# First loads of X and weights reordered onto one queue, the second weight chunk in halves, and the input norm in hooks, in a two-layer decoder step

## The chip, the cores and the metric

The kernel runs on one core of a Trainium2 chip. A core has five engines that run at the same time, each with its own instruction stream: TensorE (PE, matrix products into PSUM), VectorE (DVE), ScalarE (ACT), GpSimd (POOL) and SyncE (SP), which here only issues transfers. ACT can issue transfers too. Transfers of all queues run on the core's 16 DMA engines. The metric is the device time of one execution in microseconds; lower is better. Three runs of the kernel before took 632.65, 633.56 and 635.03 us, median 633.56.

## The reference

One inference step of a two-layer decoder, for a prompt of 256 tokens and 8 sample tokens that share the weights, so 264 columns in all. Layer 0 is block-sparse attention beside a gated mixer, layer 1 is stick-breaking attention beside a pooling mixer, and each layer ends in a feed-forward block with a short convolution. What bears on this change is the start of layer 0:

```python
def rmsnorm(x, g):
    xf = x.astype(jnp.float32)
    y = xf * lax.rsqrt(jnp.mean(xf * xf, axis=-1, keepdims=True) + EPS)
    return (y * g).astype(x.dtype)
...
    h = rmsnorm(x, norm_g)
    z = h @ w_in
    q, k, v, bu, bv = jnp.split(z, [A_WIDTH, 2 * A_WIDTH, 3 * A_WIDTH, 3 * A_WIDTH + B_WIDTH], axis=-1)
    q = rope_partial(q.reshape(B, T, A_HEADS, HEAD_DIM), pos)
    k = rope_partial(k.reshape(B, T, A_HEADS, HEAD_DIM), pos)
```

The norm's factor is one number per token, so it can be applied behind the product: the kernel multiplies X by the gain, projects, and multiplies the result by the factor R.

## The kernel before

Everything is held transposed: 128 features on the partitions, 264 tokens along the row. X is eight such tiles (`XG`, with the gain's 8 columns in front). Each weight matrix is cut into 128x128 blocks, and all blocks of the whole step lie in memory in the order in which PE uses them, as one stream of chunks: the first six chunks (0 to 5) hold 8 blocks (512 KB), all later ones 16 (1 MB). Three buffers hold chunks (`rawp`), so chunk n+3 can be loaded when chunk n has been used up.

For accuracy every product is made of three passes. A weight chunk is split, 8 blocks at a time, into a high part `wh` (a rounded copy, on ACT, L311) and a low part `wl` (the difference, on DVE, L312). X times gain is split in the same way into `xg_h` (ACT, L378) and `xg_l` (DVE, L379). A block then takes three matmuls: `wh` with `xg_h` (L334), `wh` with `xg_l` (L335), `wl` with `xg_h` (L336).

The input projection `in0` makes 20 output tiles (four each of q, k, bv, bu, v). The four q tiles go first and together: for each of the first five X tiles the four blocks of q0 to q3, then the other three X tiles for one q tile after the other. So chunk 0 is used with X tiles 0 and 1, chunk 1 with X tiles 2 and 3, chunk 2 with X tile 4 and then all the others. The four q tiles fill the four PSUM buffers `mm` of the projections. The first k tile can start only when a q tile has been evacuated, and evacuating q needs the rope factors times R (L612 to L614, then L634 to L640), so it needs the norm.

The opening. ACT issues X in four transfers (tiles 0, 1, 2 to 3, 4 to 7; L348 to L350), SP issues chunk 0 in three (2, 2 and 4 blocks; L351 to L354) and chunks 1 and 2 whole (L355, L356). Then ACT loads its function table (L357). Eight matmuls on a tile of ones, 512 columns each, keep PE at work until data is there (L358 to L362). The loop at L595 splits the three pieces of chunk 0 (`piece`, both parts on DVE, L308 and L309), makes the eight operand tiles and, two tiles behind (`SQL` 2), the squares of X for the norm (`nrm.add`: a square on ACT, L391, added up on POOL, L400 and L403). All of these are kept in the order in which they are written (`keep_in_program_order`). Behind the loop stand chunk 3, the rope table, the split of chunk 1, chunk 4, the small constants, and `nrm.finish()`: two matmuls with a matrix of ones add up the squares over the features (L411), and ACT makes R as Ln and Exp (L413, L414). Then come the three rope factors, and then the projection.

Instructions that aren't kept in order are placed by a scheduler that works on a model of the times. Within `run` (L315) hooks, small functions with a due time in units of 8 blocks, put the attention's work between the matmuls: page loads of the K cache from `KL` on (L788), score matmuls S (L654 to L657), sample scores `sc` (L456), transposes (L675), and so on. The transfers of K and V pages, of the chunks and of the small tables all go through SP's queue in one order, and a transfer whose buffer isn't free holds up all that stand behind it. Transfers also share eight completion counters in turn, so each waits for the landing of the transfer eight before it.

Of the kernel before, what the change touches and what calls it, by code (L numbers as in the profile page):

```python
# [11 lines left out]
BF16 = mybir.dt.bfloat16  # L12
I32 = mybir.dt.int32
AF = mybir.ActivationFunctionType
# [4 lines left out]
P = 128  # L19
# [18 lines left out]
KQ = 5  # L38
PINM = 8
SQL = 2  # L40
XD = (1, 2, 4, 8)
WARM = 8
YG = (2, 5)
# [19 lines left out]
MSK = 4.5  # L63
KL = 0
VL = 9
# [161 lines left out]
def tile_decoder_step(ctx: ExitStack, tc: tile.TileContext, a):  # L227
# [49 lines left out]
    NT = _NB // 8  # L277
    raws, splits = {}, {}

    def raw(ci):  # L280
        if ci not in raws:
            n = _CHUNKS[ci] * P
            r = rawp.tile([P, n], F32, tag="raw", name=f"raw{ci}")
            o = coff[ci] * P * P
            src = a["w"][o:o + P * n].rearrange("(p f) -> p f", p=P)
            raws[ci] = r
            if ci == 0:
                return lambda c, e: nc.sync.dma_start(r[:, c * P:e * P], src[:, c * P:e * P])
            nc.sync.dma_start(r, src)
        return raws[ci]  # L290
# [4 lines left out]
    def split(t):  # L295
        for tt in range(len(splits), min(t + (LOOK if pos[0] else 0), NT - 1) + 1):
            ci = chunk_of[tt]
            for c in range(ci, min(ci + 3, len(_CHUNKS))):
                raw(c)
            o = (tt * 8 - coff[ci]) * P  # L300
# [10 lines left out]
            s.activation(h, src, AF.Copy)  # L311
# [45 lines left out]
    s.preload_act_table_set("natural_log_exp_and_others")  # L357
    warm = con.tile([P, 512], BF16, name="warm")  # L358
    v.memset(warm, 1.0)
    pw = at("warm")  # L360
    for i in range(WARM):
        tc.keep_in_program_order(pe.matmul(pw, warm[:, :P], warm, start=i == 0, stop=i == WARM - 1))  # L362

    def late(dst, src):
        tc.keep_in_program_order(nc.sync.dma_start(dst, src))

# [222 lines left out]

    xg = [mv(f"xg_0{i}") for i in range(2)]  # L590
    nrm = Norm("n0", True)
    piece = split(0)
    pieces = [(0, 2), (2, 4), (4, 8)]
    for m in range(KD):
        if pieces:  # L595
            piece(*pieces.pop(0))
        operand_tile(xg[m // 4], m, X[:, m, :], GAIN[:, m:m + 1], pin=m < PINM)
        if m >= SQL:
            nrm.add(m - SQL, pin=m < PINM)
    for m in range(KD - SQL, KD):  # L600
        nrm.add(m)
    raw(3)
    late(CS, a["rope"].rearrange("p (c t) -> p c t", c=2))
    split(1)
# [7 lines left out]
    v.tensor_tensor(rope[:, 0, :], CS[:, 0, :], R, ALU.mult)  # L612
    v.scalar_tensor_tensor(rope[:, 2, :], CS[:, 1, :], SCALE, R, ALU.mult, ALU.mult)
    v.tensor_tensor(rope[:, 1, :], CS[:, 1, :], R, ALU.mult)  # L614

# [13 lines left out]
    def in0_evac(m, o):  # L629
# [11 lines left out]
        else:  # L641
            v.tensor_tensor({"v": v4, "bv": bv4, "bu": bu4}[n][:, t, :], o, R, ALU.mult)

# [424 lines left out]
```

## Time and profile before

| | |
|---|---|
| median of the three runs | 633.56 us |
| the profiled execution's own time | 632.96 us |
| its span, first to last instruction | 630.9 us |
| PE busy | 611.6 us, 97% |
| PE weight loads busy | 583.2 us, 92% |
| DVE busy | 413.2 us, 65% |
| ACT busy | 343.8 us, 54% |
| POOL busy | 82.5 us, 13% |
| mean granted PE clock | 0.994 |
| DMA | 121.42 MB, mean 192 GB/s |

Times in the profile's views are counted from the first instruction. The profiled execution took 2.06 us more than its span. "Busy" is time in which an engine had an instruction in work; "idle before" names what ended a wait, the releaser. A matmul's row lasts longer than the step to the next one, since matmuls are pipelined. Queue q1 carries SP's transfers and q10 ACT's.

### The profile page before, as it was taken

What the parts mean: (1) busy time and instruction counts of PE and PEld (TensorE: products, weight loads), DVE (VectorE), ACT (ScalarE), POOL (GpSimd) and SP (SyncE); (2) the same over time, 40 slices, a digit from 0 to 9 for tenths busy, and PEclk for the clock granted to TensorE, in tenths of its full rate; (3) what the DMA queues carried; (4) which work ended last, traced back from release to release, by engine and by line L of the source; (5) the groups of instructions that cost most, each with busy time, mean ns of one, the idle gap of its engine ahead of it and who ended that gap; (6) DMA issues with size and microseconds to landing.
All of it is one profiled execution on the core that took longest, in us unless ns stands there. A gap on an engine that the chain in (4) does not pass through costs nothing.

```text
span 630.9 us, 12406 instructions
## 1 busy us (share of the span) xinstructions
PE 611.6 (97%) x4956; PEld 583.2 (92%) x4956; DVE 413.2 (65%) x690; ACT 343.8 (54%) x608; POOL 82.5 (13%) x111
## 2 busy tenths in 40 slices
PE   7899999998999999999999999999899999999994
PEld 5887997998999999999998886999899999999994
DVE  6895674959966676655654674396996667664442
ACT  6448653667665555644442664366766555564441
POOL 3320132324000000010110000032400000001021
PEclk8999999999999999999999999999999999999998
DMA  7995673543555455795477679354355545554501
GB/s 271 324 414 223 238 262 72 182 156 132 200 201 180 161 195 198 228 382 202 179 189 300 230 117 112 129 172 169 128 200 200 179 166 191 201 165 177 200 1 70
DMA packets 40971, 121.42 MB, mean 192 GB/s; under 512 B 17490, under 2 KB 18642, under 8 KB 29522
## 3 DMA queue, kind: packets, MB, share of 16 engines
q1 hardware_dynamic: 40050, 119.15, 57.2%
q10 hardware_dynamic: 864, 1.49, 0.7%
q8 instruction: 39, 0.64, 0.4%
q14 instruction: 18, 0.15, 0.1%
HBM read 116.68 MB, written 3.94 MB: 191 GB/s over the span
## 4 chain that ended last, share of the span: by engine, by line
PE 90%; DVE 4%; ACT 2%; DMA 2%; issue 1%; POOL 1%; SPq 0%; DVEq 0%; ACTq 0%; POOLq 0%
PE mm L334 27%; PE mm L335 27%; PE mm L336 26%; DMA raw<-in_w 2%; DVE wl L312 1%; PE pv_l L470 1%; PE sc L456 1%; ACT wh L311 1%; PE Z L880 1%; PE Z L868 1%; PE pav L499 1%; DVE xn_l L379 1%; PE S L655 1%; PE S L654 1%; PE po_l L483 1%
## 5 line engine op out<-in xcount | busy, mean ns | idle before, releaser
L312 DVE TENSOR_TENSOR wl<-raw,wh 128x1024 fp32r<-128x1024 f32 x183 | 229.1, 1253 | 135.1 <-ACT wh L311 135.1
L311 ACT ACTIVATE wh<-raw 128x1024 fp32r<-128x1024 f32 x183 | 193.4, 1059 | 204.9 <-PE mm L335 187.6
L335 PE MATMUL mm<-xn_l,wh 128*128 128x264 f32 x544 | 154.4, 284 | 0.0
L336 PE MATMUL mm<-xn_h,wl 128*128 128x264 f32 x544 | 154.1, 283 | 0.0
L334 PE MATMUL mm<-xn_h,wh 128*128 128x264 f32 x544 | 153.9, 283 | 0.0
L334 PEld LDWEIGHTS mm<-xn_h,wh 128*128 128x128 f32 x544 | 102.3, 188 | 0.0
L335 PEld LDWEIGHTS mm<-xn_l,wh 128*128 128x128 f32 x544 | 102.3, 188 | 0.0
L336 PEld LDWEIGHTS mm<-xn_h,wl 128*128 128x128 f32 x544 | 102.2, 188 | 0.0
L335 PE MATMUL mm<-a_l,wh 128*128 128x264 f32 x352 | 99.9, 284 | 0.0
L336 PE MATMUL mm<-a_h,wl 128*128 128x264 f32 x352 | 99.7, 283 | 0.0
L334 PE MATMUL mm<-a_h,wh 128*128 128x264 f32 x352 | 99.5, 284 | 0.0
L335 PEld LDWEIGHTS mm<-a_l,wh 128*128 128x128 f32 x352 | 66.2, 188 | 0.0
L336 PEld LDWEIGHTS mm<-a_h,wl 128*128 128x128 f32 x352 | 66.2, 188 | 0.0
L334 PEld LDWEIGHTS mm<-a_h,wh 128*128 128x128 f32 x352 | 66.1, 188 | 0.0
L334 PE MATMUL mm<-xg_h,wh 128*128 128x264 f32 x160 | 46.9, 300 | 4.2 <-ACT wh L311 2.5
L334 PE MATMUL mm<-xg_f_h,wh 128*128 128x264 f32 x160 | 46.2, 289 | 4.5 <-DVE wk L558 4.3
L335 PE MATMUL mm<-xg_l,wh 128*128 128x264 f32 x160 | 45.6, 291 | 0.0
L336 PE MATMUL mm<-xg_f_h,wl 128*128 128x264 f32 x160 | 45.3, 283 | 0.0
L335 PE MATMUL mm<-xg_f_l,wh 128*128 128x264 f32 x160 | 45.3, 283 | 0.0
L336 PE MATMUL mm<-xg_h,wl 128*128 128x264 f32 x160 | 45.2, 294 | 0.1
L334 PE MATMUL mm<-xg_n_h,wh 128*128 128x264 f32 x128 | 37.9, 296 | 0.0
L335 PE MATMUL mm<-xg_n_l,wh 128*128 128x264 f32 x128 | 37.0, 289 | 0.0
(257 smaller groups left out, 1088.5 us busy)
## 6 DMA issues: line engine op xcount, KB each, us to landing
raw<-in_w SPq DMA_DIRECT2D x89, 1024.0 KB, 4.8
K<-in_kt SPq DMA_DIRECT2D x32, 256.0 KB, 6.2
V<-in_vp SPq DMA_DIRECT2D x32, 256.0 KB, 5.4
raw<-in_w SPq DMA_DIRECT2D x5, 512.0 KB, 5.1
CST<-in_cst SPq DMA_DIRECT2D x1, 560.0 KB, 4.7
XG<-in_x ACTq DMA_DIRECT2D x1, 528.0 KB, 7.7
out_k<-k SPq DMA_DIRECT2D x1, 528.0 KB, 8.7
out_v<-v SPq DMA_DIRECT2D x1, 528.0 KB, 3.0
```

What stands on the lines that cost most here:

```text
L311: s.activation(h, src, AF.Copy)
L312: v.tensor_tensor(l, src, h.bitcast(F32), ALU.subtract)
L334: pe.matmul(o, h[:, c:c + P], xh, start=first, stop=False)
L335: pe.matmul(o, h[:, c:c + P], xl, start=False, stop=False)
L336: pe.matmul(o, l[:, c:c + P], xh, start=False, stop=left[m] == 0)
L379: j = v.scalar_tensor_tensor(l, src, gain, h.bitcast(F32), ALU.mult, ALU.subtract)
L456: pe.matmul(ps[32 * t:32 * t + 32, :PAST].rearrange("p (g k) -> p g k", g=NPG), qz[:, t, sq, :], kt[sq][:, :, t * P:(t + 1) * P], start=sq ...
L470: pe.matmul(pv[32 * j:32 * j + 32, :], pz[:, pg, sq, :], vtiles[sq][:, pg, :], start=pg == 0, stop=pg == NPG - 1)
L483: pe.matmul(po[:, t * NS:(t + 1) * NS], msk[:, gr, 2 * t:2 * t + 2, :].rearrange("p h d -> p (h d)"), cst("selS")[:, gr * NS:(gr + 1) * NS ...
L499: pe.matmul(o, vt[:, 0, h * HD:(h + 1) * HD], w[:, :SEQ], start=True, stop=False)
L654: pe.matmul(ps[:, 0:P], qh[:, 0:P], kh[:, 0:P], start=True, stop=False, skip_group_check=True)
L655: pe.matmul(ps[:, P:384], qh[:, P:SEQ], kh[:, 0:SEQ], start=False, stop=False, skip_group_check=True)
```

## The change

All loads of the opening but one go through SP's queue, in an order written out: X tile 0 (with the gain), chunk 0 in three pieces, X tile 2, chunk 1's first half, X tile 3, its second half, X tile 4, chunk 2, X tiles 5 to 7, chunk 3. X tile 1 alone is issued by ACT, now behind its function table. Chunk 1 is split in two pieces of 4 blocks, like chunk 0's pieces; the last piece of chunk 0 and both of chunk 1 have their high part made on ACT instead of DVE. The squares follow three tiles behind the operand tiles (`SQL` 3); the last three and `nrm.finish()` with the rope factors (`norm0`) become hooks in the projection, due at 0 and 1.5. The warm-up is ten matmuls of 256 columns, and the K pages' loads start at hook 1 instead of 0 (`KL`). As built, the matmuls of the norm's sum stand on PE behind the last q matmul and ahead of the first k matmul; before, they stood between q matmuls. The first two pairs of score matmuls stand inside the fourth k tile, where they stood in the first bv tile. From the second half of the projection on, the instructions of all engines stand in the order in which they stood before.

```diff
-PINM = 8
-SQL = 2
-XD = (1, 2, 4, 8)
-WARM = 8
+SQL = 3
+WARM = 10
...
-KL = 0
+KL = 1
...
-            if ci == 0:
-                return lambda c, e: nc.sync.dma_start(r[:, c * P:e * P], src[:, c * P:e * P])
+            if ci < 2:
+                return lambda c, e: late(r[:, c * P:e * P], src[:, c * P:e * P])
...
             for c in range(ci, min(ci + 3, len(_CHUNKS))):
-                raw(c)
+                if tt > 1:
+                    raw(c)
...
-            if tt == 0:
-                def piece(c, e, h=h, l=l, src=src):
+            if tt < 2:
+                def piece(c, e, act, h=h, l=l, src=src):
                     c, e = c * P, e * P
-                    tc.keep_in_program_order(v.tensor_copy(h[:, c:e], src[:, c:e]))
+                    hh = s.activation(h[:, c:e], src[:, c:e], AF.Copy) if act else v.tensor_copy(h[:, c:e], src[:, c:e])
+                    tc.keep_in_program_order(hh)
                     tc.keep_in_program_order(v.tensor_tensor(l[:, c:e], src[:, c:e], h[:, c:e].bitcast(F32), ALU.subtract))
-                return piece
+                pieces.append(piece)
+                continue
...
-    xcut = [0] + [KD + e * T for e in XD]
-    for b, e in zip(xcut, xcut[1:]):
-        nc.scalar.dma_start(XG[:, b:e], a["x"][:, b:e])
-    part = raw(0)
-    part(0, 2)
-    part(2, 4)
-    part(4, 8)
-    raw(1)
+    def xload(m, e, eng=None):
+        b, e = KD + m * T if m else 0, KD + e * T
+        tc.keep_in_program_order((eng or nc.sync).dma_start(XG[:, b:e], a["x"][:, b:e]))
+
+    s.preload_act_table_set("natural_log_exp_and_others")
+    xload(1, 2, nc.scalar)
+    part0, part1 = raw(0), raw(1)
+    xload(0, 1)
+    part0(0, 2)
+    part0(2, 4)
+    part0(4, 8)
+    xload(2, 3)
+    part1(0, 4)
+    xload(3, 4)
+    part1(4, 8)
+    xload(4, 5)
     raw(2)
-    s.preload_act_table_set("natural_log_exp_and_others")
-    warm = con.tile([P, 512], BF16, name="warm")
+    xload(5, 8)
+    raw(3)
+    warm = con.tile([P, 256], BF16, name="warm")
...
+    split(1)
+    todo = [(0, 0, 2, False), (0, 2, 4, False), (0, 4, 8, True), None, (1, 0, 4, True), (1, 4, 8, True)]
+    def weights(n):
+        for x in [todo.pop(0) for _ in range(min(n, len(todo)))]:
+            if x:
+                pieces[x[0]](*x[1:])
+    weights(1)
     nrm = Norm("n0", True)
-    piece = split(0)
-    pieces = [(0, 2), (2, 4), (4, 8)]
     for m in range(KD):
-        if pieces:
-            piece(*pieces.pop(0))
-        operand_tile(xg[m // 4], m, X[:, m, :], GAIN[:, m:m + 1], pin=m < PINM)
+        operand_tile(xg[m // 4], m, X[:, m, :], GAIN[:, m:m + 1], pin=True)
+        weights(2 if m == 0 else 1)
         if m >= SQL:
-            nrm.add(m - SQL, pin=m < PINM)
-    for m in range(KD - SQL, KD):
-        nrm.add(m)
-    raw(3)
+            nrm.add(m - SQL, pin=True)
+        if m == 4:
+            split(2)
...
-    R = nrm.finish()
...
+    def norm0():
+        R = nrm.finish()
+        R0.append(R)
...
+    for m in range(KD - SQL, KD):
+        hk.at(0, nrm.add, m)
+    hk.at(1.5, norm0)
```

More of the change, by code (lines that the diff above doesn't have):

```diff
@@ L277, in tile_decoder_step @@
     NT = _NB // 8
-    raws, splits = {}, {}
+    raws, splits, pieces = {}, {}, []
     def raw(ci):
@@ L361, in tile_decoder_step @@
     for i in range(WARM):
-        tc.keep_in_program_order(pe.matmul(pw, warm[:, :P], warm, start=i == 0, stop=i == WARM - 1))
-    def late(dst, src):
-        tc.keep_in_program_order(nc.sync.dma_start(dst, src))
+        tc.keep_in_program_order(pe.matmul(pw[:, :256], warm[:, :P], warm, start=i == 0, stop=i == WARM - 1))
     ident = cst("ident")
@@ L608, in tile_decoder_step @@
     late(CST, a["cst"])
-    R = nrm.finish()
     rope = f4("rope")
-    v.tensor_tensor(rope[:, 0, :], CS[:, 0, :], R, ALU.mult)
-    v.scalar_tensor_tensor(rope[:, 2, :], CS[:, 1, :], SCALE, R, ALU.mult, ALU.mult)
-    v.tensor_tensor(rope[:, 1, :], CS[:, 1, :], R, ALU.mult)
+    R0 = []
+    def norm0():
+        R = nrm.finish()
+        R0.append(R)
+        v.tensor_tensor(rope[:, 0, :], CS[:, 0, :], R, ALU.mult)
+        v.scalar_tensor_tensor(rope[:, 2, :], CS[:, 1, :], SCALE, R, ALU.mult, ALU.mult)
+        v.tensor_tensor(rope[:, 1, :], CS[:, 1, :], R, ALU.mult)
     maskb0 = con.tile([P, P], BF16, name="maskb0")
@@ L641, in in0_evac @@
         else:
-            v.tensor_tensor({"v": v4, "bv": bv4, "bu": bu4}[n][:, t, :], o, R, ALU.mult)
+            v.tensor_tensor({"v": v4, "bv": bv4, "bu": bu4}[n][:, t, :], o, R0[0], ALU.mult)
     ktiles, kload = page_list(a["kt0"], "K0")
```

3 lines of the change are left out of this document (2 added, 1 removed).

## The prediction

> **What bounds the kernel now.** I read the waits of TensorE (PE) first, to see where it stands still, then the chain of waits and the order of time over the first 25 us, then the stages and the DMA counts.
>
> The order of time on PE, columns start, duration, engine, line, operation, and in brackets the idle time with its releaser:
> ```profile
> 1.46 3.60 PE L362 MATMUL warm<-warm 128*128 128x512 bf16 x8 [1.46 <-DVE warm L359]
> 4.50 0.99 PE L334 MATMUL mm<-xg_h,wh 128*128 128x264 f32 x2
> ...
> 10.81 0.76 PE L334 MATMUL mm<-xg_h,wh 128*128 128x264 f32 x4 [2.52 <-ACT wh L311]
> ...
> 18.92 0.61 PE L411 MATMUL ns_n<-acc_n,ones 128*128 128x264 f32 x2
> 19.36 0.61 PE L411 MATMUL ns_n<-sq_n,ones 128*128 128x264 f32 x2
> ...
> 22.48 0.28 PE L335 MATMUL mm<-xg_l,wh 128*128 128x264 f32 x1
> 22.60 0.28 PE L336 MATMUL mm<-xg_h,wl 128*128 128x264 f32 x1
> 24.54 0.36 PE L334 MATMUL mm<-xg_h,wh 128*128 128x264 f32 x1 [1.66 <-DVE q L636]
> ```
> PE stands still twice after its first real matmul at 4.50: 2.52 us until the second weight chunk is split, and 1.66 us at 24.54, where the first k tile wants a PSUM buffer that a q tile still holds, because its evacuation needs the norm. A matmul starts every 0.12 us (22.48 to 22.60). From 24.54 PE runs on, so all that the change can win in the opening is how far it moves that 24.54 forward.
>
> The chain of waits, columns start, duration, piece:
> ```profile
> 2.13 7.55 DMA raw<-in_w
> 9.70 1.06 ACT wh L311
> 10.76 0.41 ACT xg_h L378
> 11.17 0.31 ACT sq_n L391
> ...
> 13.33 0.95 ACT wh L311
> ...
> 16.85 3.40 DMA raw<-in_w
> 20.35 1.07 ACT wh L311
> ...
> 22.60 0.45 DVE rz_q L634 x2
> 23.04 0.32 DVE rope L612
> ...
> 24.05 0.36 DVE q L636
> 24.40 0.14 issue
> ```
> It goes by chunk 1 (landing at 9.68), ScalarE's (ACT) queue of splits and operand tiles, chunk 5 (issued at 16.85, landing at 20.25), the norm, the rope factors, the q evacuation. PE is not in it. ACT steps cost 0.41 (operand), 0.31 (square) and 0.95 to 1.06 us (split of a chunk).
>
> ACT's order of time gives the rest:
> ```profile
> 2.64 1.28 ACT L357 ACT_TABLE_LOAD   x1 [2.64 <-issue]
> ...
> 21.32 0.46 ACT L413 ACTIVATE R_n<-ns_n,epst 128x264 f32<-128x264 f32 x1
> 21.81 0.43 ACT L414 ACTIVATE R_n<-R_n 128x264 f32<-128x264 f32 x1
> ```
> The norm R is there at 22.24, 0.92 us after its first step.
>
> What the loads moved, from the DMA view of the stretches 0 to 5, 0 to 7, 0 to 9 and 0 to 10 us, one row each:
> ```profile
> DMA packets 788, 0.96 MB, mean 193 GB/s; under 512 B 71, under 2 KB 583, under 8 KB 788
> ...
> DMA packets 1003, 1.65 MB, mean 235 GB/s; under 512 B 96, under 2 KB 608, under 8 KB 1003
> ...
> DMA packets 1231, 2.47 MB, mean 275 GB/s; under 512 B 124, under 2 KB 636, under 8 KB 1231
> ...
> DMA packets 1350, 2.89 MB, mean 289 GB/s; under 512 B 141, under 2 KB 653, under 8 KB 1350
> ```
> The engines are fed at some 0.4 MB per us from 5 us on; what X and chunk 2 take, chunk 1 doesn't get.
>
> **The change part by part.** The loads first. Ahead of the end of chunk 2 the new order has X tiles 0 to 4 (5 x 0.135 MB) and chunks 0, 1 and 2 (3 x 0.524 MB), 2.25 MB. The curve passes 2.25 MB at 8.5 us. From there to the landing I add 1.2 us: X's first piece shows the short end, chunk 1 the long one.
> ```profile
> XG<-in_x ACTq DMA_DIRECT2D x1, 136.0 KB, 3.1
> raw<-in_w SPq DMA_DIRECT2D x2, 128.0 KB, 3.0
> ...
> q1 hardware_dynamic: 568, 1.05, 38.4%
> ```
> The last row is the weight queue up to 8 us: chunks 0 and 1 are 1.05 MB, moved by 8.0, seen at 9.68, so up to 1.7 us; the small pieces' 3.1 us from an issue at 0.75 end at 3.85, when 0.53 MB had been moved, some 0.6 us after their own 0.27. So chunk 2 lands between 9.1 and 10.2; I take 9.7 (11.0 before). Chunk 1's halves come by the same count at 1.2 MB and 1.6 MB, near 6.6 and 7.9. Nothing waits for them long, because ACT and VectorE (DVE) are busy with tiles 0 to 3 then.
>
> SP's queue by time:
> ```profile
> 0.75 1.34 SPq L288 DMA_DIRECT2D raw<-in_w  x3
> ...
> 3.89 0.33 SPq L289 DMA_DIRECT2D raw<-in_w  x1
> ...
> 40.02 1.47 SPq L365 DMA_DIRECT2D K<-in_kt  x2
> ```
> Up to chunk 3 it issues eleven transfers where it issued six, 0.45 us each, and a transfer waits for the landing of the one eight before it (chunk 2, the ninth, went out at 3.89, when X's first piece had landed). X tile 1 goes out on ACT's queue behind the table load, 1.28 us later: from 2.0 it lands at some 5.4, and X tile 4 on SP, with chunk 2 behind it, waits for that. By then 1.1 of 1.6 MB issued have moved, so the engines stay fed: cost nothing. If that cover were gone, it would be 1 us.
>
> Opening on PE. The first matmul stays near 4.45: it waits for the split on DVE of the first 128 KB, which is now second on its queue (issue 1.2, landing 4.1). The warm-up is 10 matmuls of 256 columns in place of 8 of 512, 2.1 us for 3.6, and ends before the weights come; that is off the path, because data set the pace. Tiles 0 and 1 (24 matmuls each) end near 8.05 and 10.95 by ACT's and DVE's order; before, tile 1 began at 10.81.
>
> Then ACT's queue binds: chunk 2's split 9.7 to 10.75, three pairs of operand tile and square, 3 x 0.72 = 2.15, to 12.9; chunk 3's split (0.95) to 13.85 (landing near 12, so not late); DVE's low half:
> ```profile
> 10.79 1.23 DVE L312 TENSOR_TENSOR wl<-raw,wh 128x1024 fp32r<-128x1024 f32 x1 [1.38 <-ACT wh L311]
> ```
> to 15.1; the 18 matmuls that stand behind it, 2.2 us, end the q projection at 17.3 (22.88 before). This is 5.6 us sooner.
>
> The hooks give part of it back. The eight squares stay where they were in ACT's order, so that part does nothing; but the column-sum matmuls, which stood between q matmuls at 18.92, now stand behind the last q matmul. So PE is done at 17.3, and then come the sum (18.92 to Ln's earliest start at 19.97, 1.05), Ln and Exp (0.92), the rope factors and the first q evacuation (23.04 to 24.54, 1.5): 17.3 + 3.47 = 20.77. The first k matmul moves from 24.54 to 20.8: 3.8 us. Chunk 5 is not late for it: it goes out when chunk 2 is free (11.95) and takes 3.4 to some 16.6 with the constants ahead of it, split by 17.6.
>
> What that costs. PE now stands still from 18.3 to 20.8, 2.5 us. The stages, columns: length, busy time of PE, PEld, DVE, ACT, POOL, the granted clock, DMA share, GB/s:
> ```profile
> 22.50:25.90 3.40, 1.74 (x15) 1.56 (x14) 2.23 (x8) 0.95 (x1) 1.58 (x2) 1.00 0.96 306
> 8.86:12.28 3.42, 1.45 (x9) 1.24 (x10) 1.98 (x3) 2.91 (x8) 1.39 (x2) 1.00 0.75 301
> 12.28:15.69 3.41, 3.41 (x18) 3.41 (x18) 3.41 (x5) 3.41 (x7) 2.96 (x4) 0.53 0.78 237
> ...
> 24.50:40.00 15.50, 15.46 (x119) 14.31 (x119) 14.14 (x33) 6.26 (x6) 5.42 (x8) 1.00 1.02 401
> ```
> With 1.45 us busy in a stretch of 3.42 the granted clock fell to 0.53 for the next 3.41; with 1.74 of 3.40 it stayed at 1.00. A gap of 2.5 us can fall on either side, by where the stretches begin. The price is 3.41 x 0.47 = 1.6 us, or 0; I take half, 0.8. Before, the same slow stretch cost nothing, as the chain ran past PE.
>
> The fourth row is the next term: after the gap DVE is busy 14.14 of 15.5 us. The changed order puts four score tiles S inside the fourth k tile, one tile sooner than before, and the K pages' loads start one hook later (KL 1 for 0). From R to k tile 0 complete the new order has three chunk splits, the rope and four q tiles on DVE, some 10.7 us, so 30.0; PE is there 8.8 us after 20.8, at 29.6. A stall of 0 to 0.8 us here and at the first transposes; it shrinks when the clock is slow. I take 0.5. The last K page is issued behind chunk 11, near 44, against 40.02 to 41.5 before:
> ```profile
> DMA to landing us min/median/max: 5.8/6.1/7.6
> ```
> These are the K pages' landings, so it comes at some 50.5, and PE asks for it at 51: nothing, and 1 us if chunk 11 slips by that much. From there the orders of all engines are as before.
>
> Sum: 3.8 - 0.8 - 0.5 = 2.5 us. The profiled execution took 632.96 (span 630.9 and 2.06 around it), so 630.5; the median of the runs shown, 633.56, is 0.6 above it: 631.1.
>
> **The rivals.** The clock stays full in the new gap. Nothing but the phase speaks for it: 1.66 us of standing still were borne, 1.95 in one stretch weren't. The gap then costs nothing, but PE meets DVE's late k tile (0.8): 3.8 - 0.8 = 3.0, 630.6. The Trainium skill, "TensorE: Matmul & The Clock Gate", Part 1, would have it so: it puts the half rate behind at least one idle window of about 3.4 us. The trace disagrees, having halved after 2.5 us of standing still; the same section's free-running window fits the stretches.
>
> The queue feeds better than my 1.2 us of lag: chunk 2 at 9.1, clock full, no stall in the middle, since DVE's chain starts sooner too. 3.8 + 0.6 = 4.4, 629.2. For it speaks the short lag of the small pieces; against it chunk 1's long one.
>
> The win is swallowed: the DVE stretch or a K page sets PE's pace until 50 us, whatever the opening does. R comes 3.0 us sooner (19.2 for 22.24), so no k tile comes sooner than that; a slow clock (1.6) and a K page some 1.4 us late take the rest: 633.5. Against it stands that PE's waits between 24.5 and 60 us show nothing so far.
>
> Slower: one queue can't carry what two did. Beside the other queue, from 5 to 6 us, q1 moved 0.16 MB; all but alone, from 9 to 10, it moved 0.41:
> ```profile
> q1 hardware_dynamic: 51, 0.16, 56.4%
> ...
> q1 hardware_dynamic: 114, 0.41, 100.2%
> ```
> If rows of 1 to 2 KB on one queue went at 0.17 MB per us, the 2.12 MB on it up to chunk 2 would need 12.5 us from 1.75 and land at 15.3, 5.6 later than I have it; the 3.8 us turn into a loss of 1.8, and the longer gaps bring 1.6 of slow clock: +3.4, 637.0. It decides from below 0.24 MB per us on. The second row speaks against it, though with rows of 4 KB. The Trainium skill, "DMA: Bandwidth & Descriptors", in its rules for kernel authors, is against it too: issuing from several engines doesn't add bandwidth, as they share the 16 engines.
>
> **How the numbers follow.** The forecast (631.1) gets 0.45, the full clock (630.6) 0.2, the better feeding (629.2) 0.15, the swallowed win (633.5) 0.12, the slow queue (637.0) 0.08. A measurement of this kernel tells 0.5%, 3.17 us, from no change: below 630.4 or above 636.7. Below lie the better feeding, some 0.07 of the full clock and 0.08 of the forecast: 0.3. Above lies most of the last, 0.07. The rest is 0.63. The range, 628.8 to 634.6, holds the first four with their spread of a microsecond.
>
> **What would show it.** Right: chunk 2 landed before 10 us, the last q matmul near 17.3, R near 19.2, the first k matmul near 20.8 with a wait for q of 2.5 us, q10 all but empty. The clock's row by stretches tells the first rival, a wait of PE for k or for S between 28 and 40 us the fourth, landings of chunk 1 after 9 us the last. It is wrong if the first k matmul comes after 23 us or before 19.

## The result, and the profile after

The changed kernel takes 635.09 us (median of 20 executions, 634.54 to 640.5), the kernel before 633.61 (20, 632.28 to 636.07); the ratio is 1.0041, 95% interval 1.0023 to 1.0059. So it is slower, by 0.4%, where 2.5 us less was forecast; the median lies 0.5 us above the range. Its executions fall into two groups: 14 at 634.5 to 636.1 (mean 635.1), 6 at 638.0 to 640.5 (mean 639.5); as the mean of all is 636.4 against 633.9 before, some half of that 2.5 us is the second group. The profiled execution, 634.58 us with a span of 632.7, is of the first.

The order of time on PE in the changed kernel (columns as in the prediction):
```profile
19.70 0.29 PE L337 MATMUL mm<-xg_h,wl 128*128 128x264 f32 x1
19.83 0.61 PE L421 MATMUL ns_n<-acc_n,ones 128*128 128x264 f32 x2
20.27 0.61 PE L421 MATMUL ns_n<-sq_n,ones 128*128 128x264 f32 x2
23.41 0.59 PE L335 MATMUL mm<-xg_h,wh 128*128 128x264 f32 x1 [2.52 <-DVE q L653]
```
The opening is better than before, but by much less than forecast: the first k matmul starts at 23.41 (24.54 before, 20.8 forecast), behind the 2.5-us wait that was foreseen. What follows costs more than that. A good marker for it is the first transpose of the sample's probabilities, pP, at the end of the first attention stretch; PE has done the same work by then in both kernels. From the view of that tile, first of before, then of after:
```profile
L711 PE MATMUL pP<-CST,psamp x2: 271/272/272, 66.7 to 66.8; 128*128 128x128 f32 x2
```
```profile
L728 PE MATMUL pP<-CST,psamp x2: 271/272/272, 68.6 to 68.7; 128*128 128x128 f32 x2
```
From the first k matmul to pP is 66.7 - 24.54 = 42.2 us before and 68.6 - 23.41 = 45.2 after. So 1.1 us are gained, 3.0 are lost, and pP comes 1.9 us later; the spans differ by 1.8, so nearly all of the loss is there by then. No wait of PE over 0.3 us stands between the two marks. A part of the 3.0 is the clock; the stages of the changed kernel (length, busy time of PE, PEld, DVE, ACT, POOL, granted clock, DMA share, GB/s):
```profile
19.50:23.00 3.50, 1.38 (x9) 0.90 (x7) 2.96 (x9) 1.79 (x3) 0.26 (x1) 0.99 0.90 298
23.00:26.40 3.40, 3.00 (x14) 3.00 (x14) 3.28 (x9) 1.64 (x2) 2.08 (x3) 0.51 1.01 407
```
A second part can be read from PE's order of time, added up by kind from each start to the next, between the marks. The projection's matmuls take 27.8 us before and 29.8 after, most of the difference being the slow clock. The scores S with their masks take 8.1 in both. The page scores take 3.9 and 4.4, the transposes 2.1 and 2.4, the samples' own scores 0.2 and 0.5: 1.1 us more for these three. What lies behind that had to be found by experiment.

Why the q projection ends at 20.0 and not at 17.3 can be read from the trace. The same stretch of the opening, 3.5 to 4.5 us, before and after (length, PE, granted clock, DMA share, GB/s):
```profile
3.50:4.50 1.00, 1.00 (x4) 1.00 1.04 365
```
```profile
3.50:4.50 1.00, 0.17 (x2) 1.00 0.58 98
```
In this microsecond the DMA engines ran half empty. By issue times it was not for want of work: nine transfers with 1.6 MB had been issued by 4.5 us, and 0.55 MB had moved. Why they ran half empty is not shown. ACT's and DVE's order of time in the changed kernel show what came of it:
```profile
9.14 0.63 ACT L307 ACTIVATE wh<-raw 128x512 fp32r<-128x512 f32 x1 [0.70 <-DMA raw<-in_w]
...
10.72 1.06 ACT L312 ACTIVATE wh<-raw 128x1024 fp32r<-128x1024 f32 x1
...
13.90 1.05 ACT L312 ACTIVATE wh<-raw 128x1024 fp32r<-128x1024 f32 x1
```
```profile
12.96 2.81 DVE L389 SCALAR_TENSOR_TENSOR xg_l<-XG,xg_h 128x264 fp32r<-128x264 f32 x3
15.70 1.77 DVE L313 TENSOR_TENSOR wl<-raw,wh 128x1024 fp32r<-128x1024 f32 x1
```
```profile
12.70 5.38 POOL L413 TENSOR_TENSOR acc_n<-acc_n,sq_n 128x264 f32<-128x264 f32 x5 [1.05 <-ACT sq_n L401]
```
Chunk 1's second half is there at 9.1 (7.9 forecast) and chunk 2 at 10.7 (issued at 5.00, 5.7 us to landing; 9.7 forecast), so ACT splits chunk 2 at 10.72 instead of 9.7. Then DVE takes 0.94 us for each low operand half and 1.77 for the split, while POOL adds squares; the forecast had 1.23 for the split. DVE ends at 17.5 instead of 15.1, and PE 2.5 us behind it.

### The profile page after: what moved, and what is told of

The parts are those of the page before. It is cut to its first block, busy times and chain, and to the rows that moved or that the text cites. A ratio compares the mean times of both kernels' runs of the same rounds, so it can differ in the third digit from the quotient of the medians.

```text
span 632.7 us, 12408 instructions
## 1 busy us (share of the span) xinstructions
PE 613.6 (97%) x4958; PEld 585.1 (92%) x4958; DVE 413.0 (65%) x690; ACT 345.0 (55%) x610; POOL 81.6 (13%) x111
## 4 chain that ended last, share of the span: by engine, by line
PE 89%; DVE 5%; issue 2%; ACT 2%; POOL 1%; DMA 1%; SPq 0%; DVEq 0%; ACTq 0%; POOLq 0%
PE mm L335 26%; PE mm L336 26%; PE mm L337 26%; DVE wl L313 1%; PE pv_l L480 1%; PE sc L466 1%; PE Z L900 1%; DMA raw<-in_w 1%; PE Z L888 1%; PE pav L509 1%; DVE xn_l L389 1%; ACT wh L312 1%; PE S L672 1%; PE S L671 1%; PE po_l L493 1%
## 5 line engine op out<-in xcount | busy, mean ns | idle before, releaser
L313 DVE TENSOR_TENSOR wl<-raw,wh 128x1024 fp32r<-128x1024 f32 x182 | 226.8, 1247 | 131.8 <-ACT wh L312 131.8
L335 PE MATMUL mm<-xg_h,wh 128*128 128x264 f32 x160 | 46.6, 302 | 3.3 <-DVE q L653 2.5
L336 PE MATMUL mm<-xg_l,wh 128*128 128x264 f32 x160 | 46.8, 297 | 0.3 <-DVE xg_l L389 0.3
```

The source lines that it names most:

```text
L313: v.tensor_tensor(l, src, h.bitcast(F32), ALU.subtract)
L335: pe.matmul(o, h[:, c:c + P], xh, start=first, stop=False)
L336: pe.matmul(o, h[:, c:c + P], xl, start=False, stop=False)
```

## The experiments

"First k" is the start of the first k matmul in the profiled execution, "to pP" the time from there to the marker, both in us; ratios are to the kernel before, measured beside. The first k matmul moves from one execution to the next by up to 0.9 us: the changed kernel with the long warm-up has it at 23.52, 24.41 and 23.52 in three profiles. So a difference of that size between two rows of this column shows nothing by itself.

| kernel | first k | to pP | median us | ratio (95%) |
|---|---|---|---|---|
| before | 24.5 | 42.2 | 633.6 | 1 |
| changed | 23.4 | 45.2 | 635.09 | 1.0041 (1.0023 to 1.0059) |
| squares' lag back | 22.3 | 45.1 | 633.57 | 1.0002 (0.9990 to 1.0013) |
| long warm-up back | 23.5 | 45.2 | 638.62 | 1.0067 (1.0047 to 1.0088) |
| lag and warm-up back | 21.7 | 43.1 | 631.78 | 0.9971 (0.9959 to 0.9982) |
| before, short warm-up | 24.2 | 42.2 | 632.78 | 0.9993 (0.9978 to 1.0008) |
| sum pinned early | 21.7 | 45.1 | 634.13 | 1.0006 (0.9994 to 1.0017) |
| order pinned | 23.6 | 44.8 | 634.55 | 1.0010 (0.9995 to 1.0025) |
| order pinned, gap filled | 23.3 | 43.2 | 633.59 | 1.0010 (0.9993 to 1.0027) |
| lag, warm-up, order of before | 21.8 | 43.4 | 632.15 | 0.9982 (0.9968 to 0.9996) |
| loads and hooks (KL 0) | 22.2 | 42.7 | 631.21 | 0.9970 (0.9961 to 0.9980) |
| loads alone | 21.6 | 42.1 | 630.37 | 0.9958 (0.9945 to 0.9971) |
| loads alone, heads in pairs | 21.7 | (40.3) | 628.39 | 0.9924 (0.9905 to 0.9944) |

**Which part of the change: the squares' lag, or the warm-up.** Four kernels. The first sets the lag back:
```diff
-SQL = 3
+SQL = 2
```


> The changed kernel with one constant set back: the squares of the input again run two tiles behind the operands (SQL 2 instead of 3). The order that the planner writes changes with it: the column sum of the squares stands three quarters of a tile before the end of the q projection instead of behind its last matmul, and the score matmuls of the first four heads stand together at 8.71 tiles instead of at 7.04 and 7.33. Theory 'lag' (the sum behind the projection, and the attention matmuls strewn over it, are what the change lost): first k matmul near 22.0 us (23.41 in the changed kernel), its wait under 1.5 us (2.52), the rows from it to the first pP matmul back near 42.2 us (45.15), so 1.5 to 4 us less than the changed kernel: 631.5 to 633.5. Rival 'clock' (the short warm-up alone lost it): under 0.7 us less. Rival 'VectorE beside GpSimd' (the operands of the second half are late because VectorE slows while GpSimd adds): the q projection ends near 20.0 us as before, and under 0.7 us less.

Measured: 633.57 us, 1.0002. Its PE order, and two rows of the stages (length, PE, granted clock, DMA share, GB/s):
```profile
17.79 0.61 PE L421 MATMUL ns_n<-acc_n,ones 128*128 128x264 f32 x2
...
22.32 0.36 PE L335 MATMUL mm<-xg_h,wh 128*128 128x264 f32 x1 [1.29 <-DVE q L653]
```
```profile
20.00:24.00 4.00, 2.71 (x23) 1.00 0.94 364
24.00:28.00 4.00, 4.00 (x36) 1.00 1.01 406
```
One constant takes the loss away: the sum stands between q matmuls again, the gap is 1.29 us, the clock stays full and the longest execution took 634.71. But my theory expected the stretch to pP to come back to 42.2, and it stayed at 45.1, now without any slow clock. That part of it fell; the order is taken up below.

The warm-up alone, in the changed kernel:
```diff
-WARM = 10
+WARM = 8
...
-    warm = con.tile([P, 256], BF16, name="warm")
+    warm = con.tile([P, 512], BF16, name="warm")
...
-        tc.keep_in_program_order(pe.matmul(pw[:, :256], warm[:, :P], warm, start=i == 0, stop=i == WARM - 1))
+        tc.keep_in_program_order(pe.matmul(pw, warm[:, :P], warm, start=i == 0, stop=i == WARM - 1))
```


> The changed kernel with the warm-up of the kernel before (8 matmuls of 512 columns, not 10 of 256). The order on TensorE stays that of the changed kernel. Theory 'lag': the matmuls of the first tile run fast from near 5.6 us instead of 9.2, but the operands of the later tiles bind, so q ends within 0.5 us of 20.0 and the time is within 0.7 us of the changed kernel's, 634.4 to 635.8. Rival 'clock': the time falls by 1.5 us or more, to 633.6 or less, because the raised clock and the later half-rate window both shift.

Measured: 638.62 us, as 6 of 10 executions are of the second group; the lowest is 634.36. The expected 634.4 to 635.8 holds, rounded, for three of the other four, not for the median. The first k matmul is at 23.5 and the stretch 45.2 long, as in the changed kernel. So the short warm-up is not what the change lost. The kernel also shows that DVE sets the end of the q projection: the first 24 matmuls are done 0.7 us sooner (9.03 for 9.75), and q ends at 20.1 all the same, 2.5 us behind DVE's last split (17.59). In the profile with the first k matmul at 24.41, DVE is done at 18.38 and q at 20.9, again 2.5 us behind.

Both together, by these two edits:

> The changed kernel with both: squares two tiles behind, and the long warm-up. The order on TensorE: column sum at 3.25 tiles, scores of heads 0 to 3 from 7.58 to 8.46. If the two effects are separate and 'lag' carries the most, this is within 0.7 us of the kernel with the squares alone set back. If 'clock' carries it, it is as fast as the one with the warm-up alone.

Measured: 631.78 us, 0.9971, better than either kernel. The expectation that it would stay within 0.7 us of the lag alone fell: it is 1.8 us below. The two profiled executions are 2.2 us apart. In them 0.6 is the first k matmul (21.7 for 22.3), within its scatter, and 2.0 the stretch to pP, which the scheduler (the planner of the expectations) ordered in another way.

And the short warm-up in the kernel before, by the same lines the other way round:

> The kernel before with the shortened warm-up alone (10 matmuls of 256 columns, not 8 of 512). The order on TensorE is that of the kernel before but for the column sum, an eighth of a tile sooner. Theory 'lag': the first tiles run at half rate until about 9 us, but they wait for loads, so within 0.7 us of the kernel before (632.9 to 634.3). Rival 'clock': 1 to 2 us slower (634.6 to 635.6), and the executions near 639 us that the changed kernel shows appear here too.

Measured: 632.78 us, 0.9993, the same as before, with the first k matmul 0.4 us sooner. So in the kernel before, the short warm-up costs nothing that can be told from no change, as the prediction had it.

**Where the sum stands.** The sum alone is moved, with the lag and the warm-up of the change: the matmuls of q's last blocks and the sum are kept in written order, the sum behind block 25, and the q evacuations wait for it in the program.
```diff
-            pe.matmul(p[:, :T], ones, x, start=i == 0, stop=i == len(parts) - 1)
+            y = pe.matmul(p[:, :T], ones, x, start=i == 0, stop=i == len(parts) - 1)
+            if name == "n0":
+                tc.keep_in_program_order(y)
...
-    hk.at(1.5, norm0)
+    hk.at(2.25, norm0)
```


> The changed kernel (short warm-up, squares three tiles behind) with only the column sum moved: its two matmuls are pinned three quarters of a tile before the end of the q projection. The planner's order of the attention matmuls moves with it, and is that of the kernel with the squares two tiles behind. Theory 'the sum stands too late': first k matmul near 22.3 us (23.41 in the changed kernel), no half-rate window behind it, and 633 to 634 us, within 0.5 us of the kernel with the squares set back; the rows from the first k matmul to the first pP stay near 45 us, since their order is as strewn. Rival 'the squares themselves': the sum waits for them at its new place, TensorE stands still there, first k matmul at 23.0 us or later and 634.5 us or more.

Measured: 634.13 us, 1.0006, highest 635.1; 45.1 us to pP. The first k matmul in it:
```profile
21.67 0.39 PE L337 MATMUL mm<-xg_h,wh 128*128 128x264 f32 x1 [0.35 <-DVE q L664]
```
The granted clock is 1.00 from 20 to 28 us. So it is the place of the sum, not the squares, that delays R and opens the gap.

**The order and the gap.** The first attempt fixed PE's order from the very first weight matmul on: the attention's matmuls are kept in program order, and their hooks set to where the kernel before has them.
```diff
+    QKT = (8.25, 8.25, 8.25, 8.25, 10, 10, 10.5, 10.625)
+    TRT = (9.25, 9.375, 10, 10.375, 11, 11.25, 12, 12.875)
...
-        hk.at(SQK + h // 2, s_qk, h)
-        hk.at(STR + h // 2, s_tr, h)
+        hk.at(QKT[h] - 1, s_qk, h)
+        hk.at(TRT[h] - 1, s_tr, h)
...
-    hk.at(SC0, sm_score, 0)
+    hk.at(8.25, sm_score, 0)
```


> The changed kernel with the sum left behind the last q matmul, and TensorE's order from there to the first pP pinned to that of the kernel before: scores of heads 0 to 3 together at 8.25 tiles, page scores at 9.25 and 10, and so on. Theory 'strewn order costs 1.6 us': first k matmul still near 23.4 us with its 2.5 us wait and a half-rate window behind it, rows from there to pP near 43.5 us (45.15), so near 633.2 us, and still executions 4 to 5 us longer. Rival 'the half-rate window is all of it': rows near 45.1 us and 634.6 us or more.

The same with the gap filled:
```diff
+        for i in range(14):
+            tc.keep_in_program_order(pe.matmul(pw[:, :256], warm[:, :P], warm[:, :256], start=i == 0, stop=i == 14 - 1))
```


> As the kernel with the pinned order, and 14 spare bf16 matmuls of 256 columns, whose result nothing reads, pinned behind the column sum, so that TensorE isn't idle for 2.5 us there (about 1.6 us of it are filled). Theory 'the gap drops the clock': no half-rate window behind the first k matmul, rows to pP near 42.2 us, near 631.8 us, and no executions 4 to 5 us longer. Rival 'the clock window comes anyway': within 0.4 us of the kernel with the pinned order alone.

And with everything that had helped, the edits of lag, warm-up, early sum and order together, without the fill:

> All that helped, together: loads of the changed kernel, squares two tiles behind, the sum pinned at 3.25 tiles, the long warm-up, and TensorE's order of the kernel before. Theory: first k matmul near 21.7 us, rows to pP near 42.2 us, so 2.8 us less than the kernel before, near 630.8 us. Rival 'something after the first pP gives it back': not under 631.8 us, that of the kernel with the squares and the warm-up set back.

Measured: 636.96, 635.98 and 634.64 us (1.0045, 1.0043, 1.0011); every theory was missed. The experiment had changed too much: with the q matmuls in written order the sum of the first of them stood at 21.2 instead of 19.8, and with page scores grouped while page loads begin a hook later (KL 1) PE waited for a page. The row of PE's waits in the first of them, columns total, times, longest:
```profile
PE sc L470 <- DMA K<-in_kt: 2.0, 1, 2.0
```
So these three tell nothing on the order. The second of them tells something on the clock. The fill kept it full behind the gap, but it fell at 40 us and stayed down to 46.8 (length, PE, granted clock, DMA share, GB/s):
```profile
38.00:39.00 1.00, 0.72 (x5) 1.00 1.07 387
39.00:40.00 1.00, 1.00 (x7) 1.00 1.10 381
40.00:41.00 1.00, 1.00 (x4) 0.51 1.01 422
```
In the 3.4 us before that, PE stood still for 0.28 us only; the rest was score matmuls S. So a half-rate piece can come with hardly any waiting ahead of it.

The order was tried again, pinned only from the first k matmul on, the page loads as before, and the page scores split as in the kernel before:
```diff
-KL = 1
+KL = 0
...
+    hk.at(9, sm_score, 1, (4,))
+    hk.at(9, s_qk, 4)
+    hk.at(9, s_qk, 5)
+    hk.at(9, s_tr, 2)
+    hk.at(9, sm_score, 1, (5, 6, 7))
```


> The changed kernel with nothing but the same pinned order and page loads as before; the sum stays behind the last q matmul and the warm-up short. Theory 'strewn order': first k matmul near 23.4 us, half-rate window behind it, rows to pP near 43.6 us (45.15), 633.3 us. Rival 'order is no term': 634.6 us or more.

> As that, with 14 spare matmuls of 256 columns behind the column sum whose result nothing reads. Theory 'the gap drops the clock': no half-rate window from 22 to 28 us, rows near 42.3 us, 632.0 us. Rival: a half-rate window comes later all the same, as it did at 40 to 47 us in the kernel with the whole order pinned and the fill, and nothing is gained.

Measured: 634.55 and 633.59 us. The fill in the second, in PE's order of time, and the same stretch of the two kernels, first without the fill, then with it (length, PE, granted clock, DMA share, GB/s):
```profile
20.64 1.69 PE L636 MATMUL warm<-warm 128*128 128x256 bf16 x14
23.33 0.39 PE L337 MATMUL mm<-xg_h,wh 128*128 128x264 f32 x1 [0.99 <-DVE q L661]
```
```profile
23.50:26.90 3.40, 3.30 (x15) 0.50 1.01 385
```
```profile
23.50:26.90 3.40, 3.40 (x29) 1.00 1.02 387
```
With 1.69 us of the gap filled the half rate is gone, and the stretch to pP falls from 44.8 to 43.2: the gap's price is 1.6 us where it is paid. In the whole time the two can't be told apart (both 1.0010), and the theories' 633.3 and 632.0 us were missed by 1.3 and 1.6. The order alone gave 0.4 us of the stretch instead of the 1.6 expected: before's order, run on data that come sooner, takes 43.2 without the slow clock, not 42.2. The same pinned order on the kernel with lag and warm-up back (`SQL` 2, 8 matmuls of 512 columns):

> The changed kernel with the squares two tiles behind and the long warm-up, page loads as before (KL 0), and TensorE's order pinned from the first k matmul on to that of the kernel before (the q projection and the sum stay the planner's). Theory 'each way in and out of the page scores costs about 0.25 us': first k matmul near 21.7 us, rows from it to the first pP near 42.2 us (43.10 with the planner's own order), 630.9 us. Rival 'the order of before fits only the times of before': TensorE waits for the scores' k and p tiles instead, rows at 43 us or more, 631.8 us or more.

Measured: 632.15 us, 43.4 to pP, no better than the planner's own order (631.78, 43.1). The time is the rival's (43 us or more, 631.8 or more), but not for its reason: PE waited 0.4 us once, for a weight split, and not for the scores' tiles. So the order of before is no better here than the planner's own.

**POOL beside DVE.** POOL's adds of the squares are left out, so that the norm sums only the first and the last square.
```diff
+            elif self.name == "n0" and self.acc is not None:
+                pass
```


> The changed kernel without GpSimd's six adds of the squares of the input: the norm then sums only the first and the last square, so R, and with it q, k and all that follows, is another (left out on purpose: the work, not the time around it). Theory 'VectorE slows beside GpSimd': the low halves of the operands (L389) take 0.49 us each (0.94 with the adds), the split of the third chunk 1.23 us (1.77), and the last q matmul ends near 17.6 us instead of 20.0. Rival 'ScalarE and the loads set it': VectorE's instructions shorten, but the last q matmul ends after 19 us all the same.

DVE's order of time in it:
```profile
13.99 1.30 DVE L389 SCALAR_TENSOR_TENSOR xg_l<-XG,xg_h 128x264 fp32r<-128x264 f32 x3
16.00 1.23 DVE L313 TENSOR_TENSOR wl<-raw,wh 128x1024 fp32r<-128x1024 f32 x1 [0.71 <-ACT wh L312]
```
0.43 for 0.94 us, 1.23 for 1.77: the adds cost DVE 2.05 us here (2.81 + 1.77 - 1.30 - 1.23). The Trainium skill, "GPSIMD Engine Reference", section 1, names a cause: POOL's path to memory is shared with VectorE, for instructions with two inputs from SBUF, which both of these are; the trace agrees. But q ended at 20.4, not at 17.6, so on the end of the projection the rival's number (after 19) was met. In this execution chunk 1's second half was split at 10.16, 1.0 us later than in the changed kernel, and PE's order differs (the sum's first matmul at 13.5). What the adds cost the end of the projection is left open.

**The second group of executions.** No profile had caught one, so the two kernels that show it were profiled again.

> The changed kernel unaltered, profiled again. Its executions fall into two groups, 634.5 to 636.1 us and 638.0 to 640.5 us (6 of 20), and the profiled one was of the first. Theory 'the 2.5-us gap costs the clock more than one window in some executions': an execution of the second group shows two or more half-rate windows behind the first k matmul (near 23 us), one after the other. Rival 'another place': the extra half-rate time stands elsewhere, in the attention stretch (as from 40 to 47 us and from 54 to 61 us in the two kernels with the whole order pinned) or behind 70 us. An execution of the first group tells nothing new.

> The changed kernel with the long warm-up, profiled again: 6 of its 10 executions were at 638 to 640 us. Theory and rival as for the changed kernel profiled again.

> The same once more, for an execution of the second group: theory, half-rate windows in a row behind 23 us; rival, elsewhere.

The first was caught: 639.18 us, span 637.3. The others, 635.67 and 634.74, were of the first group and show the half rate behind the gap. PE's order of time and the stages (length, PE, granted clock, DMA share, GB/s) of the changed kernel's long execution:
```profile
23.39 0.39 PE L335 MATMUL mm<-xg_h,wh 128*128 128x264 f32 x1 [2.53 <-DVE q L653]
...
33.93 0.48 PE L671 MATMUL S<-k,q 64*128 64x128 f32 x2 [1.42 <-DVE k L657]
```
```profile
26.00:36.00 10.00, 8.58 (x67) 1.00 0.92 334
36.00:36.50 0.50, 0.50 (x6) 0.86 0.83 295
36.50:46.50 10.00, 10.00 (x57) 0.50 0.81 311
46.50:47.00 0.50, 0.50 (x5) 0.90 0.00 0
```
The theory fell and the rival holds. Here the gap of 2.53 us cost no clock at all. So PE came 1.3 us sooner to the first score matmul S, at 32.5, which this order puts inside the fourth k tile. There it stood 1.42 us for DVE's k. In the execution of the first group, with the slow clock behind the gap, the same matmul starts at the same time:
```profile
33.94 0.49 PE L671 MATMUL S<-k,q 64*128 64x128 f32 x2
```
So up to here the two cost the same, and DVE sets the time: it finishes the k tile 12.0 us after R, at 33.8, in both. From there they differ: in the long execution the clock falls at 36.4 and stays at half for 10.2 us, through the scores and the page scores. The stretch to pP is 49.7 us long, 4.6 more than in the first group, which is about the distance of the two groups. So in these two profiles the changed kernel pays either for the gap or behind the early S. That the wait for k brought the half rate on is not shown: this is one execution, and the fill above had a half-rate piece behind S with 0.28 us of waiting. The kernel that lets S come later (order pinned, 12 executions) and those with the sum early show none above 636; the first two pinned kernels, with S as late, do (640.16 and 643.44), the former's profile with its half rate from 54 to 61 us, behind the wait for the page.

**Which part is worth something.** The loads alone, with lag, warm-up and page loads (KL 0) back and the norm written ahead of the projection:
```diff
+    for m in range(KD - SQL, KD):
+        nrm.add(m)
+    norm0()
...
-    for m in range(KD - SQL, KD):
-        hk.at(0, nrm.add, m)
-    hk.at(1.5, norm0)
```


> Only the first part of the change: loads on one queue in TensorE's order, second chunk in halves, its split on ScalarE. The norm is written ahead of the projection as before, squares two tiles behind, the long warm-up, page loads as before. Theory 'the loads carry the gain': first k matmul near 21.8 us, no half-rate window, and within 0.7 us of the kernel with squares and warm-up set back (631.8). Rival 'the hooks carry it': first k matmul near 23 us or later, 633 us or more.

The same without these lines, so with the hooks of the change:

> The same with the norm in hooks. Theory 'the loads carry the gain': within 0.5 us of the kernel without the hooks, and of the kernel with KL 1. Rival 'the hooks carry it': 1 us or more faster than without them.

Measured: 630.37 us without the hooks, 631.21 with them. So the loads carry the whole gain of this version, 0.9958; the hooks bring nothing, and may cost 0.8 us, though the intervals overlap. The theory's sizes were off: 1.4 us from the kernel with lag and warm-up back instead of at most 0.7, and 0.8 between the two instead of at most 0.5. The first k matmul is at 21.64, 2.9 us sooner than before, in the one profile.

Its trace also showed why an order can be quick. Score matmuls of before, one head at 38.25 and the next at 39.32, and of the kernel with the loads alone:
```profile
38.25 0.49 PE L654 MATMUL S<-k,q 64*128 64x128 f32 x2
38.57 0.59 PE L655 MATMUL S<-k,q 64*128 64x256 f32 x2
...
39.32 0.48 PE L654 MATMUL S<-k,q 64*128 64x128 f32 x2
```
```profile
32.96 0.50 PE L675 MATMUL S<-k,q 64*128 64x128 f32 x4
33.28 0.61 PE L676 MATMUL S<-k,q 64*128 64x256 f32 x4
33.72 0.49 PE L675 MATMUL S<-k,q 64*128 64x128 f32 x4
33.94 0.70 PE L676 MATMUL S<-k,q 64*128 64x256 f32 x4
...
34.97 0.22 PE L678 MATMUL S<-maskb,identb 128*128 128x128 bf16 x1
```
Where the planner put two heads' matmuls alternately, four of them took the 0.50 us that two take alone: four heads in 2.2 us, not 4.3 (4 x 1.07). The other way, the kernel with the lag set back has its page scores cut up by transposes:
```profile
46.14 0.27 PE L692 MATMUL pt<-CST,p 128*128 128x128 f32 x1
...
46.47 0.62 PE L466 MATMUL sc<-K,qz_l 128*32 128x256 f32 x2
47.02 0.44 PE L692 MATMUL pt<-CST,p 128*128 128x128 f32 x2
47.39 0.62 PE L466 MATMUL sc<-K,qz_l 128*32 128x256 f32 x4
47.94 0.33 PE L692 MATMUL pt<-CST,p 128*128 128x128 f32 x1
```
Two or four rows of page scores hold PE for 0.55 us in such a place (46.47 to 47.02, 47.39 to 47.94), where the kernel before runs 32 of them in 1.93:
```profile
44.18 1.93 PE L456 MATMUL sc<-K,qz_l 128*32 128x256 f32 x32
```
The first of these two findings was tested by writing every pair of heads alternately:
```diff
+        for i in range(4):
+            for h, ps in pss.items():
...
+                if PINFIRST or i or h > h0:
+                    tc.keep_in_program_order(y)
```
`PINFIRST` is False, so the first matmul of a pair stays the planner's.

> The kernel with the loads alone (630.4 us), and the score matmuls of heads 2t and 2t+1 written alternately, matmul by matmul. In its trace the planner had done so for heads 0 to 3 (four heads in 2.1 us from 32.96 us; the kernel before has 1.07 us for each head), not for heads 4 to 7. Theory 'two heads side by side take the time of one, since they lie in different halves of the partitions': heads 4 to 7 save up to 2 us too, 628.4 to 629.6 us. Rival 'what made heads 0 to 3 quick is something else': within 0.5 us of 630.4 us.

Measured: 628.39 us (628.01 to 629.05), 0.9924 (0.9905 to 0.9944), 2.0 us less than the loads alone. In it pP stands one tile, 24 matmuls, further on, at 64.8; at 0.12 us each that is 2.9 us, so to the same point it is some 40.3, an estimate. Heads 0 to 3 take about 2.2 us as they did; heads 4 to 7 save 1.1 us, as the S rows of the stretch, from start to start, sum to 4.9 us for 6.0. The other 0.9 stands mostly in the page scores and transposes, whose order moved too, so not all of the 2.0 us is the alternation. The Trainium skill, "TensorEngine Tiling (Array Packing)", Overview, has it so: with 64 rows of contraction two independent tiles fit, up to twice as fast; the trace agrees (0.50 us for four as for two). This is the fastest version that was run. The second finding, the cut-up page scores, was not tested by itself.

## Why the prediction was wrong

Point by point, in its own steps.

- *The loads, "the engines stay fed: cost nothing", 1 us if that cover were gone.* The loads came a microsecond late: 98 GB/s from 3.5 to 4.5 us, chunk 1's second half 1.2 us late, chunk 2 1.0 us late. That is the size of the bound, but by luck: the reason that the prediction gave for it, X tile 1 held by the table load, didn't occur (its transfer was issued at 0.77 us). What was wrong is the curve of bytes moved, taken from the kernel before: 0.67 MB by 5 us for 0.96, and 2.25 MB near 9.7 for 8.5. The lag from there to the landing, 1.2 us in the prediction, was 1.0.
- *DVE's low half to 15.1.* This is the largest miss on the way to the first k matmul. The durations were taken from rows without POOL's adds beside them; the profile before had the slower ones too (four low halves from 11.93 us in 3.19, three splits from 15.05 in 4.60). DVE was done at 17.5: 1.0 from ACT's later start, the other 1.4 from its own slower work. So the q projection ended at 20.0 instead of 17.3.
- *From the end of q to the first k matmul, 3.47 us.* Right: 19.99 to 23.41, 3.42. So the first k matmul is 2.6 us late by the two steps above, past the 23 us from which the prediction called itself wrong, and the change won 1.1 us there, not 3.8.
- *"The hooks" put the sum behind q.* The place was right, the cause wrong: with the lag set back and the hooks left, the sum is early again (17.79). So it was the planner's answer to the longer lag, not the hook, that put the sum there.
- *The clock, 0 or 1.6 us, taken as 0.8.* Both happened, in different executions, and the price is 1.6 where it is paid by itself (44.8 against 43.2, order pinned). Halving it was no forecast for either. In the changed kernel it is no term of its own: the first S starts at 33.94 with the slow clock and at 33.93 without, as the next step holds PE there.
- *A stall of 0 to 0.8 us on DVE's k, since S stands a tile sooner.* That it shrinks when the clock is slow was right. Its size was wrong: DVE needed 12.0 us from R to the k tile (21.85 to 33.8), not 10.7, two of its chunk splits at 1.2 us and one at 1.8. Where the clock stayed full the stall was 1.42 us, and the half rate further on cost 4.6 us. The first rival, "the clock stays full" at 630.6 us, names just this meeting, but priced it at 0.8: the case that I held to be cheaper is the dear one. The fourth rival, DVE setting PE's pace, came in this one place.
- *The rest of the stretch to pP.* Nothing was set down for it beside that stall, and it cost 1.4 us (3.0 less the 1.6 of the clock), 1.1 of it in page scores, transposes and the samples' own scores. The prediction took the order of matmuls of several kinds to be free as long as PE doesn't wait. Across the kernels above the stretch takes from 42.1 to 45.1 us, without a wait over half a microsecond and at full clock. That 1.1 us is the price of this order is read from the trace; no run changed that order alone.
- *Short warm-up off the path, and from the second half on as before.* Right: 0.9993 for the first; 1.9 us at pP and 1.8 at the end for the second.

Sum for the first group, against the forecast gain of 2.5: 2.7 less at the first k matmul (1.1 for 3.8), 0.8 more for the clock (or for the stall that takes its place), 0.9 more for stall and order (1.4 for 0.5) make -1.9, and the spans say -1.8. So the loads' part of the mechanism was right and mis-sized, while what turned the sign is the stretch behind it: the gap or the early S, and the order of PE. Of the rivals, the slow single queue didn't come, though its sign, chunk 1 after 9 us, was met by 0.1 us: 2.12 MB had gone through q1 by 9.7 us, 0.27 MB per us from 1.75 on, where that rival needed less than 0.24, and chunk 2 landed at 10.7, not 15.3. On the clock the Trainium skill's rule ("TensorE: Matmul & The Clock Gate", Part 1: half rate behind one idle window of about 3.4 us) is not borne out: a gap of 2.5 us was enough in the profiled execution, while one of 2.53 us cost nothing in the long one, where the clock fell 2.4 us behind a wait of 1.42.

## What to carry to other kernels

When a planner orders the instructions, a constant off the path (here how far the squares lag) can reorder the busy engine; so compare the built orders, and price the switches between kinds of matmul, not only the waits. Take a duration from rows where the same neighbours run, above all for DVE beside POOL. And before work is taken off a path, ask what the engine will then reach too early: here it met a wait of 1.4 us at a new place, and in one execution 10 us at half clock followed.

## What the runs showed of the hardware that was not expected

- The half rate came in pieces of 3.4 us: one behind the gap, three in a row (36.36 to 46.6 us, by the 0.86 and 0.90 of the edge rows) behind the early S, two in a row (39.98 to 46.8) in the first kernel with the fill. Counting back from 36.36 by 3.41, an estimate, a window ended at 22.7 in the long execution and held 1.86 us of the gap; in the profiled one it ended at 22.9 and held 2.05. That would explain why the one dropped and the other didn't. It does not explain the drop at 36.36, where the window before held 1.0 us of standing still (32.95 to 33.93) and 2.0 us of score matmuls, nor the one at 39.98, behind 0.28 us of standing still and 3.0 us of score matmuls. Both would fit if these, on half the rows, counted for less; that is not shown.
- A filled gap kept the clock behind it: 14 matmuls of 256 columns, 1.69 us, whose result nobody reads.
- Alternating the matmuls of two heads that lie in different halves of the partitions halves their time where all of a pair's matmuls alternate (four heads in 2.2 us for 4.3). Writing all eight heads in pairs took 2.0 us off the whole, 1.1 of them in these matmuls.
